# One layer of a hybrid diffusion network on one core: branch rows stored unsplit, the first stage in a written order over all token groups, and the sums of rows behind the context's modulation

## The chip, the cores and the metric

The kernel runs on one core of a Trainium2 chip. The metric is the device time of one execution in microseconds (us). The core's engines are the tensor engine (PE in the profile, with its weight loads shown apart as PEld), the vector engine (DVE), the scalar engine (ACT), GpSimd (POOL) and the sync engine (SP), which here only issues DMAs. ACT and POOL issue DMAs too, in line with their other work; the profile calls these queues SPq, ACTq and POOLq.

## The reference

One layer (DEPTH is 1, D is 1024) is computed for 1024 latent tokens, which lie on a grid 64 wide, and 256 context tokens, 1280 rows in all, with the same weights. Cut to what matters:

```python
sh1, sc1, gt1, sh2, sc2, gt2 = jnp.split(silu(cond) @ w_ada + b_ada, 6, axis=-1)   # one row per stream
u    = rmsnorm(x, g_norm1) * (1 + sc1) + sh1
xp, su, sv, q, k, v, o_pre, gate_pre, br_pre = jnp.split(u @ w_in, points, axis=-1)
y_a  = pool_branch(xp, w_pool, pool_scale, grid)      # window means, minus x, 4 channel groups
y_b  = sgu_branch(su, sv, g_sgu, w_sgu, b_sgu)        # su * (w_sgu @ rmsnorm(sv) + b), chunks of 128
y_c, C_out, n_out, m_out = mlstm_branch(q, k, v, o_pre, gate_pre, ...)   # 4 heads of 128, two directions
branches = jnp.einsum('btrc,rcd->btrd', jnp.stack([y_a, y_b, y_c], axis=2), w_branch)
merged   = jnp.sum(sigmoid(br_pre).reshape(B, T, 3, D) * branches, axis=2)
x  = x + gt1 * (merged @ w_out)
u2 = rmsnorm(x, g_norm2) * (1 + sc2) + sh2
x  = x + gt2 * (jnp.square(relu(u2 @ w_ff1)) @ w_ff2)  # hidden width 4096
return rmsnorm(x, g_final) for both streams, C_out, n_out, m_out of the context
```

All is float32.

## The kernel before

**Products in parts.** Nearly every float32 operand of PE is split into a high half (a cast to a shorter format, `fp32r` in the profile) and a low half (the value less the high half). A product then takes three matmuls: high by high, high by low, low by high (`dense`, `product`). A split is a cast, on ACT or DVE, and a subtraction, on DVE unless said otherwise: `load_w` for a weight of 128x1024, `put_split` for activations, `load_half` and `split` later in the kernel.

**Tokens and tiles.** Tokens form three groups: 0 and 1 are 512 latent tokens each, 2 is the 256 context tokens. Activations lie as 128 channels by up to 512 tokens, in 59 slots of 128x512 (`slot`), with a few rings of smaller count: five tiles `tmp` in the first half of the kernel, and from the gating on the rings `first4`, `six`, `ring` and `tmp2` (four, six, six and six tiles). A ring's tile is handed out again when its last reader is done, so a write into it can wait. `xt[i]` are the ten row tiles of 128 tokens.

**Stages** (times from the start of the span):

- 0 to 92: four blocks of `w_ada` are split and multiplied with the conditioning vectors (`mod_split`), and turned to columns (`mod_cols`), which gives `sh1` and `a1`. The rows are normalised (`norm_rows`: two squarings on ACT, then small steps, among them a power on POOL, then in `scale_rows` one multiplication on DVE), transposed on PE (`transpose_cols`, in the written order `tr(k)` for k from 0 to 7) and modulated on ACT (`modulate_cols`, `mc(k)`). Each modulated tile of groups 0 and 1 is stored to DRAM (`scr_u`) and split. k and v of head 0 for group 0 run in between (tiles `p_k`, `p_v`).
- 92 to 142: the products of the gates (tiles `pg`, weights `wg`), and behind them a chain of small steps on DVE and ACT on 36 rows of 1280 (from L331 to L411, `dmb`), which the four heads need. k, v and q of head 0 run beside it (`head_proj(0)`).
- 142 to 465: four heads. `head(h)` is the matrix memory of one head; `head_proj(h + 1)` is emitted behind it. Each head leaves three tiles `yc` (three groups), stored to `scr_yc` (L582 to L587).
- 465 to 590: pooling (`pool_project`, `pool_window`, `pool_out`) and spatial gating (`spatial`), which leave `ya` and `yb` in the same way (L698 to L701 and L757 to L761).
- 590 to 886: twelve pairs of branch gates, each as seven products of quarters in place of eight (`GatePair`). Their stores go to `scr_g`. Beside them `mod_piece` gathers the rest of the modulation: sums on DVE, a reduction over partitions on POOL, tiles `acc` out of `tmp2`.
- 886 to 1060: the branch products in the order 1, 0, 2 of the branches (loop from L963, products L986 to L988): the rows of a branch are read back, the gates (`sg`) are read back, weights come by `load_half`.
- 1060 to 1210: `project_out` (L1104 to L1110), `modulate_ff(g)` for the three groups (normalise, transpose, modulate for the second half; L1070 to L1084) and `context_out(0..3)`. `quarter_sums(raw2q, ...)` (L715) takes differences of quarters of the modulated rows in place; `split_sum` splits them.
- 1210 to the end: sixteen pairs of the feed-forward's first product (`FeedPair`), then its second (L1340 to L1342).

**What sets the order.** Most of the program goes through a planner, which rearranges the instructions of each engine by modelled times. Instructions issued through `Pinned`, and those in `keep_in_program_order`, keep the written order on their engine:

```python
V, A, G, PE = (Pinned(tc, e) for e in engines)   # from here: written order
...
    V, A, G, PE = engines                        # from here: the planner
```

Before, the pinned part ends behind k and v of head 0 for group 0. Groups 1 and 2, the gates and all that follows are the planner's. DMAs that are issued from `SP` are the planner's too, throughout; those of the modulated tiles are issued from pinned ACT:

```python
        if g < 2:
            A.dma_start(scr_u[g][k], val)
```

The low halves of `w_ada` are made on DVE, but for two of each eight, which POOL makes (`POOL_LO = (2, 5)`). Before, branch rows are split where they are made, stored as halves from ACT, and read as halves into their slots by SP.

Of the kernel before, what the change touches and what calls it, by code (L numbers as in the profile page):

```python
# [14 lines left out]
P = 128  # L15
# [3 lines left out]
T = 1280  # L19
# [10 lines left out]
POOL_LO = (2, 5)  # L30
# [19 lines left out]
def hybrid_step(  # L50
# [100 lines left out]
    scr_ya = dp.tile([2, H, P, T], F32, name="scr_ya")  # L151
    scr_yb = dp.tile([2, H, P, T], F32, name="scr_yb")
    scr_yc = dp.tile([2, H, P, T], F32, name="scr_yc")
# [23 lines left out]
    def modulate_cols(dst, ps, g, k, a, sh, name):  # L177
# [3 lines left out]
        if g < 2:  # L181
            A.dma_start(scr_u[g][k], val)
# [37 lines left out]
    def mod_split(b, ks=range(KT), behind=2):  # L220
# [26 lines left out]

    V, A, G, PE = (Pinned(tc, e) for e in engines)
    scale_rows(0)
    u0 = [None] * KT  # L250

    def tr(k):
        u0[k] = transpose_cols(xt[0:4], 0, k, "u")

    def mc(k):
        modulate_cols(uT, u0[k], 0, k, a1, sh1, "u")

    mod_split(0)
    mod_split(2, (0, 1))
    mod_cols(0)  # L260
# [9 lines left out]
    mod_split(1, (4, 5))  # L270
    mc(1)
    tr(3)
    mod_split(1, (6, 7))
    ps_k0 = ps_mm("p_k00")
    dense(ps_k0, w_k0, uT, 0, (0,))
    mc(2)
    mod_split(3, (0, 1))
    mod_cols(1)
    mod_split(3, (2, 3))
    dense(ps_k0, w_k0, uT, 0, (1,))  # L280
    tr(4)
    tr(5)
    tr(6)
    mod_split(3, (4, 5, 6, 7))
    mc(3)
    w_v0 = load_w(None, "v0", raw_v0)
    mod_cols(3)
    dense(ps_k0, w_k0, uT, 0, (2, 3))
    tr(7)
    ps_v0 = ps_mm("p_v00")  # L290
    dense(ps_v0, w_v0, uT, 0, (0, 1, 2, 3))
# [6 lines left out]
    wgh = wp.tile([P, KT, 100], F32R, tag="hi", name="wg_hi", bufs=NHL)  # L298
    wgl = wp.tile([P, KT, 100], F32R, tag="lo", name="wg_lo", bufs=NHL)
    for i in range(2):  # L300
        ks = slice(4 * i, 4 * i + 4)
        tc.keep_in_program_order(A.copy(wgh[:, ks], wg[i]))
        tc.keep_in_program_order(V.tensor_tensor(wgl[:, ks], wg[i], wgh[:, ks].bitcast(F32), ALU.subtract))
    for i in range(4, NT):
        SP.dma_start(xt[i], xs[i])
    for g in (1, 2):
        scale_rows(g)
        t0, n = GROUPS[g]
        for k in range(KT):
            modulate_cols(uT, transpose_cols(xt[t0 // P : (t0 + n) // P], g, k, "u"), g, k, a1, sh1, "u")  # L310
# [5 lines left out]
    G.dma_start(bgt, bg)  # L316
    G.dma_start(m0t, m0)
    G.dma_start(sel, sel8)
# [3 lines left out]
    for g in range(3):  # L322
        t0, n = GROUPS[g]
        pg = ps_sd(f"pg{g}")
        for k in range(KT):
            ahi, alo = uT[k][g]
            PE.matmul(pg[0:100, :n], wgh[:, k, :], ahi, start=k == 0, stop=False)
# [129 lines left out]
    def proj(idx, name, evict, eng=V):  # L457
        w, ps = begun.pop(name, (None, None))
        w = w or load_w(w_in[idx], name, eng=eng)
        for g in range(3):  # L460
            if ps is None or g > 0:
                ps = ps_mm(f"p_{name}{g}")
                dense(ps, w, uT, g)
            evict(g, ps)
# [1007 lines left out]
```

## Time and profile before

| | |
|---|---|
| median of three runs | 1978.72 us |
| lowest, highest | 1972.24, 1979.62 us |
| time of the profiled execution | 1978.97 us |
| its span, first to last instruction | 1977.2 us |
| mean granted PE clock over the span | 0.99 |
| packets of DMA, bytes | 160382, 328.45 MB |

The span is what the profile shows; the 1.8 us beside it lie around it. In the profile's rows, a line is that of the kernel above; `out<-in` are tiles by name; `x` stands for a count. A matmul or another operation that was issued through `Pinned` has the line of that helper, L44, whatever function wrote it, so such rows are told apart by their tiles. Rows of the timeline begin with the start and the duration in us, and end, in brackets, with how long the engine had been idle and what released it. The granted clock is the share of full speed that PE was given.

### The profile page before, as it was taken

How to read it: one execution, taken by the hardware profiler on the slowest of the kernel's cores; microseconds unless marked ns; L12 is line 12 of the kernel's file. 1: busy time of each engine (PE TensorE's matmuls, PEld its weight loads, DVE VectorE, ACT ScalarE, POOL GpSimd, SP SyncE). 2: the span in 40 equal slices, each digit the busy share in tenths (PEclk: the TensorE clock that was granted, in tenths of full speed). 3: DMA queues.
4: the chain of work that ended last, by engine and by line, in shares of the span. 5: the costliest groups of instructions: out<-in, count | busy, mean ns of one | idle time of the engine just before them, and what ended most of it. 6: DMA issues, size and time to landing. Idle time of an engine off the chain costs nothing.

```text
span 1977.2 us, 28274 instructions
## 1 busy us (share of the span) xinstructions
PE 1916.4 (97%) x10160; PEld 1634.8 (83%) x10160; DVE 1321.5 (67%) x2221; ACT 846.1 (43%) x1732; POOL 383.1 (19%) x372
## 2 busy tenths in 40 slices
PE   5999999999899999999999999999999999999997
PEld 2688888998778888878888888888888878888886
DVE  6684344448878979773566489788876655644664
ACT  6543454653133333331113365545455545443433
POOL 3000001116402324330000005444531110000002
PEclk9999999999999999999999998999999999999999
DMA  8211111112564545359743335777774586655544
GB/s 343 86 46 38 49 59 42 40 57 81 181 224 144 176 139 179 130 194 360 260 129 118 118 123 181 279 257 254 260 262 139 185 322 209 212 169 151 165 133 150
DMA packets 160382, 328.45 MB, mean 166 GB/s; under 512 B 18672, under 2 KB 45168, under 8 KB 158192
## 3 DMA queue, kind: packets, MB, share of 16 engines
q1 hardware_dynamic: 107024, 220.10, 33.9%
q10 hardware_dynamic: 38976, 52.97, 7.4%
q0 software_dynamic: 14240, 53.56, 7.3%
q8 instruction: 80, 1.31, 0.3%
q14 instruction: 62, 0.51, 0.1%
HBM read 225.34 MB, written 101.22 MB: 165 GB/s over the span
## 4 chain that ended last, share of the span: by engine, by line
PE 54%; DVE 3%; issue 1%; ACT 0%; DMA 0%; POOL 0%; ACTq 0%; POOLq 0%; SPq 0%; DVEq 0%
PE w L1340 6%; PE w L1342 6%; PE w L1341 6%; PE fT L830 3%; PE fT L828 3%; PE fT L829 3%; PE pb L986 3%; PE pb L987 3%; PE pb L988 3%; PE fB L830 2%; PE fB L828 2%; PE fB L829 2%; PE po L1104 2%; PE po L1106 2%; PE po L1105 2%; PE fc L828 1%
## 5 line engine op out<-in xcount | busy, mean ns | idle before, releaser
L1179 POOL TENSOR_TENSOR z<-z 128x512 f32<-128x512 f32 x64 | 99.0, 1547 | 122.6 <-DMA z<-in_w_ff 120.1
L885 DVE TENSOR_TENSOR z<-z 128x512 f32<-128x512 f32 x112 | 96.3, 860 | 2.5
L445 POOL PARTITION_ALL_REDUCE acc<-acc x16 | 54.0, 3413 | 188.3 <-DVE acc L439 117.7
L439 DVE SCALAR_TENSOR_TENSOR acc<-z,scond,acc 128x512 f32<-128x512 f32 x112 | 86.0, 816 | 0.0
L1294 POOL TENSOR_TENSOR rs_y<-rs_y,neghalf 128x1 f32<-128x1 f32 x10 | 9.4, 939 | 333.6 <-DVE rs_y L1293 333.5
L1145 ACT ACTIVATE z<-z 128x512 f32<-128x512 f32 x64 | 40.4, 632 | 66.8 <-DVE z L894 31.3
L910 ACT ACTIVATE z<-z 128x512 f32<-128x512 f32 x48 | 30.2, 632 | 72.2 <-DVE z L894 27.5
L819 ACT CAST hi_wb<-raw_wb 128x512 fp32r<-128x512 f32 x24 | 14.8, 621 | 100.1 <-PE pb L987 66.2
L131 POOL TENSOR_TENSOR rs_h<-rs_h,neghalf 128x4 f32<-128x4 f32 (+1 forms) x12 | 11.9, 991 | 207.5 <-DVE rs_h L130 207.4
L992 DVE TENSOR_TENSOR sg<-pb,sg 128x512 f32<-128x512 f32 (+1 forms) x48 | 28.8, 601 | 31.5 <-PE pb L988 31.4
L582 DVE SCALAR_TENSOR_TENSOR yc<-th,ccol,z 128x512 f32<-128x512 f32 (+1 forms) x12 | 7.9, 661 | 57.2 <-PE th L580 57.2
L1146 ACT ACTIVATE z<-z 128x512 f32<-128x512 f32 x64 | 40.3, 629 | 1.1
L1107 DVE TENSOR_TENSOR po<-po,gt 128x512 f32<-128x512 f32 (+1 forms) x24 | 14.6, 607 | 35.5 <-PE po L1106 35.4
L670 POOL TENSOR_TENSOR z<-z 128x1024 f32<-128x1024 f32 (+13 forms) x20 | 34.8, 1750 | 14.1 <-ACT z L654 12.7
L446 POOL TENSOR_TENSOR acc<-acc,bt 1x512 f32<-1x512 f32 x16 | 25.9, 1631 | 58.6 <-issue 58.6
L1170 POOL DMA_DIRECT2D scr_s<-x x48 | 26.4, 550 | 55.6 <-DVE x L1164 49.6
L1110 ACT ACTIVATE po<-z 128x512 f32<-128x512 f32 (+1 forms) x24 | 12.7, 529 | 48.4 <-DVE z L1109 34.1
L44 PE MATMUL pm<-wah,shl 128*4 128x512 f32 x32 | 14.9, 485 | 16.7 <-DVE s_x L44 12.8
L516 DVE SCALAR_TENSOR_TENSOR z<-z,dmb,kv 128x129 f32<-128x129 f32 x56 | 16.3, 345 | 21.9 <-PE kv L505 21.6
L569 DVE TENSOR_TENSOR den<-den,gcol 128x2 f32<-128x2 f32 x40 | 6.2, 159 | 35.2 <-ACT den L568 34.5
L993 DVE TENSOR_TENSOR z<-z,sg 128x512 f32<-128x512 f32 (+1 forms) x48 | 28.8, 601 | 1.3
L990 DVE TENSOR_TENSOR z<-pb,sg 128x512 f32<-128x512 f32 (+1 forms) x24 | 14.1, 600 | 22.1 <-PE pb L988 17.7
(5093 smaller groups left out, 7311.5 us busy)
## 6 DMA issues: line engine op xcount, KB each, us to landing
z<-in_w_ff SPq DMA_DIRECT2D x64, 512.0 KB, 5.4
z<-in_w_ada SPq DMA_DIRECT2D x64, 256.0 KB, 3.1
scr_t<-z POOLq DMA_DIRECT2D x16, 1024.0 KB, 4.6
z<-in_w_in SPq DMA_DIRECT2D x24, 512.0 KB, 4.4
scr_g<-z ACTq DMA_DIRECT2D x48, 256.0 KB, 2.0
sg<-scr_g SPq DMA_DIRECT2D x48, 256.0 KB, 4.5
scr_h<-z ACTq DMA_DIRECT2D x48, 256.0 KB, 3.9
scr_s<-x POOLq DMA_DIRECT2D x48, 256.0 KB, 3.3
```

Source lines behind the costliest of these rows:

```text
L439: V.scalar_tensor_tensor(acc[j], raw, scond[:, k, j : j + 1], acc[j], ALU.mult, ALU.add)
L828: PE.matmul(ps, whi[:, s], ahi, start=first and k == ks[0], stop=False)
L829: PE.matmul(ps, whi[:, s], alo, start=False, stop=False)
L830: PE.matmul(ps, wlo[:, s], ahi, start=False, stop=end and k == ks[-1])
L885: V.tensor_tensor(out, x, y, op)
L986: PE.matmul(pb[:, :n], whi[:, s], yh, start=kc == 0, stop=False)
L987: PE.matmul(pb[:, :n], whi[:, s], yl, start=False, stop=False)
L988: PE.matmul(pb[:, :n], wlo[:, s], yh, start=False, stop=kc == 3)
L1179: G.tensor_tensor(out, x, y, ALU.subtract)
L1340: PE.matmul(banks[j], h_[:, s], rh, start=fp == 0, stop=False)
L1341: PE.matmul(banks[j], l_[:, s], rh, start=False, stop=False)
L1342: PE.matmul(banks[j], h_[:, s], rl, start=False, stop=fp == NFP - 1)
```

## The change

1. `scr_ya`, `scr_yb`, `scr_yc` hold one copy of each row, unsplit. The three places that make them store one tile each, from SP. Each branch reads its twelve tiles into `tmp2` and splits them there, with a cast on ACT and a subtraction on DVE.
2. `POOL_LO` goes: DVE makes all low halves of `w_ada`. The stores of the modulated tiles are issued from POOL's queue.
3. `scale_rows` becomes `row_stats` and `row_apply`. The loads of row tiles 4 to 7 come ahead of those of the gate weights; row tiles 8 and 9, the gate weights and q's weight of head 0 are fetched within the pinned part.
4. The pinned part is written in another order and runs on over groups 1 and 2: transpositions four steps ahead of the products, modulations two ahead, and k, v and q of head 0 as the products. The gate products of groups 0 and 1 stand ahead of the steps of group 2, those of group 2 last. `proj` and `head_proj` take up what is then begun; the gate weights' halves move from the weight rings into slots.
5. `quarter_sums(raw2q)` runs whole behind `modulate_ff(2)`; before, its first half stood between `context_out(2)` and `context_out(3)`.

The products, their number and their shapes are the same. The diff, cut:

```diff
-POOL_LO = (2, 5)
...
-    scr_ya = dp.tile([2, H, P, T], F32, name="scr_ya")
+    scr_ya = dp.tile([H, P, T], F32, name="scr_ya")
...
         if g < 2:
-            A.dma_start(scr_u[g][k], val)
+            nc.gpsimd.dma_start(scr_u[g][k], val)
...
-    def scale_rows(g):
-        for i in range(GROUPS[g][0] // P, (GROUPS[g][0] + GROUPS[g][1]) // P):
-            r = norm_rows(xt[i], 1, f"x{i}")
-            V.tensor_scalar(xt[i], xt[i], r[:, 0:1], None, ALU.mult)
+    def row_stats(i):
+        row_rstd[i] = norm_rows(xt[i], 1, f"x{i}")
+
+    def row_apply(i):
+        V.tensor_scalar(xt[i], xt[i], row_rstd[i][:, 0:1], None, ALU.mult)
...
-    wg = [slot(f"wg{i}", F32)[:, 0:400].rearrange("p (k c) -> p k c", c=100) for i in range(2)]
-    for i in range(2):
-        SP.dma_start(wg[i], w_gate[:, 4 * i : 4 * i + 4, :])
+    for i in range(4, 8):
+        SP.dma_start(xt[i], xs[i])
...
-            (G if k in POOL_LO else V).tensor_tensor(wl, ada[b, k], wh.bitcast(F32), ALU.subtract)
+            V.tensor_tensor(wl, ada[b, k], wh.bitcast(F32), ALU.subtract)
...
     mod_split(0)
-    mod_split(2, (0, 1))
-    mod_cols(0)
+    mod_split(2)
+    w_k0 = load_w(None, "k0", raw_k0)
+    raw_q0 = fetch_w(w_in[I_Q], "q0")
...
     tr(0)
     tr(1)
     tr(2)
-    mod_split(2, (2, 3, 4, 5, 6, 7))
-    mod_split(1, (0, 1))
+    mod_split(1, (0, 1, 2))
+    mod_cols(0)
     mod_cols(2)
-    mod_split(1, (2, 3))
-    w_k0 = load_w(None, "k0", raw_k0)
+    mod_split(1, (3,))
     mc(0)
...
     for k in (4, 5, 6, 7):
-        mc(k)
+        if k < 6:
+            mc(k + 2)
+            row_apply(k)
+        if k == 4:
+            row_stats(7)
         dense(ps_k0, w_k0, uT, 0, (k,))
         dense(ps_v0, w_v0, uT, 0, (k,))
-    begun = {"k0": (w_k0, ps_k0), "v0": (w_v0, ps_v0)}
-    V, A, G, PE = engines
...
+    row_apply(6)
+    row_apply(7)
+    w_q0 = load_w(None, "q0", raw_q0)
...
+    begun = {nm: (w, []) for nm, w in (("k0", w_k0), ("v0", w_v0), ("q0", w_q0))}
+    ps_q0 = ps_mm("p_q00")
+    dense(ps_q0, w_q0, uT, 0, range(0, 4))
+    steps = [(g, k) for g in (1, 2) for k in range(KT)]
+    for k in range(4):
+        tr(k, 1)
+    mc(0, 1)
+    mc(1, 1)
+    dense(ps_q0, w_q0, uT, 0, range(4, 8))
+    for at, (g, k) in enumerate(steps):
...
+        if (g, k) == (2, 0):
+            gates_of(0)
+            gates_of(1)
+        if at + 4 < len(steps):
+            tr(steps[at + 4][1], steps[at + 4][0])
+        if at + 2 < len(steps):
+            mc(steps[at + 2][1], steps[at + 2][0])
+        if k == 0:
+            begun["k0"][1].append(evict_kqv("k", 0, g - 1, ps_k0, kq0))
+            begun["v0"][1].append(evict_kqv("v", 0, g - 1, ps_v0, kq0))
...
+        dense(ps_k0, w_k0, uT, g, (k,))
+        dense(ps_v0, w_v0, uT, g, (k,))
...
+    gates_of(2)
+    V, A, G, PE = engines
...
-            part = [tmp(f"yc{h}_{g}_{i}", F32R)[:, :n] for i in range(2)]
-            put_split(part, yc[:, :n])
-            for i in range(2):
-                A.dma_start(scr_yc[i, h, :, t0 : t0 + n], part[i].bitcast(F32))
+            SP.dma_start(scr_yc[h, :, t0 : t0 + n], yc[:, :n])
...
-            part = [tmp(f"ya{gi}_{g}_{i}", F32R)[:, :n] for i in range(2)]
-            sc = ccol[:, C_PS + gi : C_PS + gi + 1]
-            A.activation(part[0], ps[:, :n], AF.Copy, scale=sc)
-            V.scalar_tensor_tensor(part[1], ps[:, :n], sc, part[0].bitcast(F32), ALU.mult, ALU.subtract)
-            for i in range(2):
-                A.dma_start(scr_ya[i, gi, :, t0 : t0 + n], part[i].bitcast(F32))
+            ya = tmp(f"ya{gi}_{g}")
+            A.activation(ya[:, :n], ps[:, :n], AF.Copy, scale=ccol[:, C_PS + gi : C_PS + gi + 1])
+            SP.dma_start(scr_ya[gi, :, t0 : t0 + n], ya[:, :n])
...
-            part = split_part(f"yb{ci}", g)
-            put_split(part, mix[g][:, :n])
-            for i in range(2):
-                A.dma_start(scr_yb[i, ci, :, t0 : t0 + n], part[i].bitcast(F32))
+            SP.dma_start(scr_yb[ci, :, t0 : t0 + n], mix[g][:, :n])
...
-                part = split_part(f"y{r}_{kc}", g)
-                for i in range(2):
-                    SP.dma_start(part[i].bitcast(F32), scr[i, kc, :, t0 : t0 + n])
-                ys[kc].append(part)
+                raw = tmp2(f"yr{r}_{kc}_{g}")
+                SP.dma_start(raw[:, :n], scr[kc, :, t0 : t0 + n])
+                hi, lo = split_part(f"y{r}_{kc}", g)
+                A.copy(hi, raw[:, :n])
+                V.tensor_tensor(lo, raw[:, :n], hi.bitcast(F32), ALU.subtract)
+                ys[kc].append((hi, lo))
...
-    quarter_sums(raw2q, (0, 1))
     context_out(3)
...
     modulate_ff(2)
-    quarter_sums(raw2q, (2, 3))
+    quarter_sums(raw2q)
```

More of the change, by code (lines that the diff above doesn't have):

```diff
@@ L313, in hybrid_step, with evict_kqv @@
+    row_apply(7)
+    w_q0 = load_w(None, "q0", raw_q0)
+    kq0 = slot("kq0", F32)
+    def evict_kqv(nm, h, g, ps, kq):
+        n = GROUPS[g][1]
+        if g == 2 and nm != "v":
+            t = kq[:, 0:256] if nm == "k" else kq[:, 256:512]
+        else:
+            t = slot(f"{nm}T{h}_{g}", F32)
+        A.activation(t[:, :n], ps[:, :n], AF.Copy, scale=float(P) ** -0.5 if nm == "k" else 1.0)
+        return t
     bgt = cp.tile([36, 2], F32, name="bgt")
@@ L455, in hybrid_step, with proj @@
     hn2 = [z[:, 9010 + i * 512 : 9522 + i * 512].rearrange("p (c t) -> p c t", t=P) for i in range(2)]
-    def proj(idx, name, evict, eng=V):
-        w, ps = begun.pop(name, (None, None))
+    def proj(idx, name, evict, eng=V, w=None, groups=range(3)):
         w = w or load_w(w_in[idx], name, eng=eng)
[L460 to L463, printed above, removed]
+        for g in groups:
+            ps = ps_mm(f"p_{name}{g}")
+            dense(ps, w, uT, g)
             evict(g, ps)
```

123 lines of the change are left out of this document (69 added, 54 removed).

## Prediction

> **What bounds the kernel now.** I read the page's totals first, then the time by stage, then what the tensor engine (PE) waited for, then the order of time where it waited.
>
> ```profile
> span 1977.2 us, 28274 instructions
> PE 1916.4 (97%) x10160; PEld 1634.8 (83%) x10160; DVE 1321.5 (67%) x2221; ACT 846.1 (43%) x1732; POOL 383.1 (19%) x372
> ```
>
> ```profile
> 12.80:60.00 47.20, 39.84 (x180) 22.77 (x181) 36.95 (x60) 32.48 (x63) 13.53 (x12) 0.93 0.80 313
> 60.00:92.00 32.00, 27.67 (x141) 19.29 (x140) 19.03 (x48) 14.36 (x30) 2.43 (x4) 1.00 0.17 66
> 92.00:142.00 50.00, 47.20 (x264) 41.19 (x262) 42.91 (x47) 24.24 (x28) 2.47 (x5) 0.93 0.15 46
> 142.00:490.00 348.00, 347.05 (x2265) 315.70 (x2265) 169.93 (x433) 169.78 (x484) 50.05 (x42) 1.00 0.16 53
> 490.00:600.00 110.00, 99.95 (x514) 82.46 (x513) 84.34 (x122) 33.88 (x57) 25.99 (x28) 0.97 0.54 188
> 860.00:900.00 40.00, 37.81 (x179) 31.67 (x178) 21.22 (x30) 11.72 (x21) 11.54 (x7) 0.96 0.82 273
> 900.00:1150.00 250.00, 250.00 (x1261) 213.16 (x1260) 140.53 (x245) 56.81 (x114) 8.52 (x15) 1.00 0.54 190
> 1150.00:1215.00 65.00, 59.88 (x390) 54.68 (x389) 60.47 (x124) 46.52 (x99) 16.87 (x8) 0.92 0.36 125
> ```
>
> The columns of the stages are the stretch, its length, then busy time of PE, its weight loads, DVE, ACT and POOL, the granted clock, the DMA share and GB/s. PE is the bound, 97% busy, and the change adds and removes no product: every gain has to come out of PE's 60.8 us of idle time (1977.2 less 1916.4) and out of the stretches at half clock. Of the idle time 12.8 us lie before the first product, and after it the change touches five places: 7.4 us up to 60, 4.3 up to 92, 2.8 up to 142, 10.1 in the pooling and gating stage (490 to 600), 2.2 where the branch products begin, 5.1 around the sums. From 142 to 490 and from 900 to 1150 PE has no idle time worth naming.
>
> ```profile
> PE pm L44 <- ACT wah L44: 3.9, 1, 3.9
> PE p_su L124 <- ACT xp L639: 3.4, 1, 3.4
> PE pt L1078 <- ACT xn L1070: 3.0, 1, 3.0
> PE fB_g L828 <- ACT a_g0h L810: 2.6, 1, 2.6
> 32.00:40.00 8.00, 4.33 (x14) 1.92 (x15) 6.09 (x10) 4.20 (x8) 1.28 (x1) 0.57 1.03 414
> 520.00:528.00 8.00, 4.75 (x14) 3.75 (x15) 3.82 (x7) 5.01 (x9) 1.89 (x1) 0.79 0.40 140
> ```
>
> The waits are single and short, 2.6 to 3.9 us, but behind them the clock falls to half: 43% and 21% of 8 us are missing in the last two rows, 3.4 and 1.7 us, and 7% of the 50 us from 92 to 142, 3.5 us. Where PE works in that time it is lost too, so a wait of 3 us is worth about 5.
>
> **First stage, token group 0** (to 60 us).
>
> ```profile
> 12.15 5.74 ACT L44 CAST wah<-wa 128x512 fp32r<-128x512 f32 x10
> 29.03 0.57 ACT L44 COPY mrow_hi<-pm 4x512 f32<-4x512 f32 x1 [1.68 <-PE pm L44]
> 31.55 0.78 ACT L44 ACTIVATE val_u<-pt_u,sh,a 128x512 f32<-128x512 f32 x1
> 34.60 0.35 ACTq L44 DMA_DIRECT2D scr_u<-val_u  x1
> 35.00 1.14 ACT L44 CAST wah<-wa 128x512 fp32r<-128x512 f32 x2 [2.67 <-DMA wg<-in_w_gate]
> 36.04 0.77 ACT L44 ACTIVATE val_u<-pt_u,sh,a 128x512 f32<-128x512 f32 x1
> 59.38 0.39 PE L44 MATMUL p_v<-u7h,lo_v 128*128 128x512 f32 x1
> L44 DVE TENSOR_TENSOR wal<-wa,wah 128x512 fp32r<-128x512 f32 x24 | 20.4, 904 | 1.3 <-ACT wah L44 1.3
> L44 POOL TENSOR_TENSOR wal<-wa,wah 128x512 fp32r<-128x512 f32 x8 | 11.3, 1412 | 20.1 <-ACT wah L44 19.8 <-PE pt_u L44 0.3
> L44 DVE TENSOR_TENSOR u3l<-val_u,u3h 128x512 fp32r<-128x512 f32 x1 | 0.7, 693 | 0.0
> L1170 POOL DMA_DIRECT2D scr_s<-x x48 | 26.4, 550 | 55.6 <-DVE x L1164 49.6
> ```
>
> The value of 31.55 is ready at 32.33, yet its store leaves ACT's queue at 34.60: it waited there for an earlier load, 2.67 us, and the next casts, the second modulation (36.04) and PE's 3.9 us stand behind it. The change takes these stores off ACT. Its new list up to the second modulation is 21 casts of 0.574 from 12.15 (24.2), the cast of w_k0 (1.1 as two of them), two row copies (1.1) and the first modulation (0.8): 27.3; plus the 2.5 us that before lie between the second row copy (29.03) and the modulation it releases (31.55): 29.8 in place of 36.04, 6.2 us earlier.
>
> All 32 low halves now fall to DVE. That is 8 more by 0.693, 5.5 us; but the 24 it had cost 904 ns beside POOL and 693 is what the same shape costs alone, so 24 x 0.211 = 5.1 us come back: nil. The 8 POOL instructions of 1412 ns go. What is moved ahead of the stage's end is row work of group 1: four statistics (ACT, in its idle time) and two row multiplications of 1024 columns on DVE, 2.8 us as four subtractions. The loads of rows 4 to 7 move ahead of those of the gate weights in SP's queue; the gate products come after group 1, so this costs nothing, unless the rows land late, and then at most what the row work was moved ahead by. 59.8 - 6.2 + 2.8: the last product of group 0 ends 3.4 us earlier, at 56.4.
>
> The 16 stores cost POOL 0.55 each (the row of scr_s): 8.8 us in an engine busy 13.5 of 47 us, of which the 11.3 above go; but the powers that scale the rows now queue among them. On what they do to DVE and back, the Trainium skill, "SBUF — State Buffer", section "SBUF: two separate sides", holds against this edit: a store issued from GpSimd cannot write its descriptors while DVE runs in a two-port mode, 0.62 us becoming some 3.1 us. By that figure the 8 stores of group 0 would be an estimated 25 us of POOL. The 550 ns mean of the 48 scr_s stores doesn't show it, and I go by that row.
>
> **Groups 1 and 2, the products of head 0, the gates.**
>
> ```profile
> 24.22 1.53 PE L44 MATMUL pt_u<-cst,z 128*128 128x128 f32 x12
> 92.13 0.28 PE L124 MATMUL p_k<-u0c,hi_k 128*128 128x256 f32 x1
> 94.44 0.42 DVE L331 COPY z<-pg 36x256 f32<-36x256 f32 x1
> 103.34 0.40 PE L124 MATMUL p_q<-u0h,hi_q 128*128 128x512 f32 x1
> 108.81 0.39 PE L124 MATMUL p_q<-u0h,hi_q 128*128 128x512 f32 x1
> 142.17 0.32 DVE L411 COPY dmb<-pd 128x160 f32<-128x160 f32 x1
> ```
>
> 24 products of 512 columns take 5.47 us (103.34 to 108.81), 0.228 each; k of group 2 with v of groups 1 and 2 takes 11.21 (92.13 to 103.34), so a 256-column product is 0.12. Between 59.8 and 92 PE had 72 of the first (16.4), 24 of the second (2.9) and 48 transpositions of 0.13 (6.1): 25.4 of 32.2 us, 6.8 lost, to rows not yet scaled and to modulations. In the new order rows 4 to 7 are scaled in advance, transpositions run four ahead and modulations two, and q0's 24 products stand between. For each k PE has six products and four transpositions, 1.9 us, DVE a cast and a subtraction, 1.1, ACT one modulation, 0.8: PE is the slowest. I leave 1.8 us of waits, for lo_q0 behind two row multiplications and for the evictions behind the gate products: 5 us gained, with the 3.4 above 8.4. By then PE has also done the 11.21 and 5.47 us, 16.7, that used to follow the gates. The gates so end at about 92.1 + 16.7 - 8.4 = 100.4. **I take 8.5 us**, with bounds of 2 (only ACT's stalled store goes) and 16 (all 7.4, 4.3 and the half clock).
>
> Against it stands the chain of small gate steps on DVE and ACT: 94.44 to 142.5, 48 us, before head 0 can be transposed. PE covered it with the 16.7 us and with the rest of q0 and o0. Now the chain starts at 102 and the cover is the rest of q0 (5.47 + 2.9), o0, and k, v of head 1 (13.8 each): 49.8 us. It suffices if the planner brings in head 1's products. The idle 2.8 us and the half clock of this stretch are a matter of where it puts the gate's transpositions. **I take 1 us gained**; from 5 (both gone) to a loss of 29 (only q0 and o0 as cover, 26 idle, 3.4 at half clock).
>
> **Rows stored unsplit.**
>
> ```profile
> L699 DVE SCALAR_TENSOR_TENSOR ya<-pp,ccol,ya 128x512 fp32r<-128x512 f32 (+1 forms) x12 | 7.9, 658 | 4.5 <-ACT ya L698 4.5
> 523.25 0.50 PE L124 MATMUL p_su<-u0h,hi_su 128*128 128x512 f32 x1 [3.39 <-ACT xp L639]
> 521.59 0.93 ACTq L701 DMA_DIRECT2D scr_ya<-ya  x2
> 522.62 0.58 ACT L639 COPY xp<-p_xp 128x512 f32<-128x512 f32 x1 [1.71 <-DVE mt L750]
> ```
>
> Of 72 stores 36 are left, on SP instead of ACT. In the pooling stage 12 DVE subtractions (7.9 us) and the 12 casts with 12 subtractions of the yb rows go, the latter at most 0.693 each and the casts less: some 20 of DVE's 84 us. What PE gets is one place: at 522.62 ACT copies out a finished product only after the stores queued ahead of it (521.59) have left, and PE waits 3.4 us and then runs at half clock, 5.1 in all. **I take 4**; 8.6 if the wait of fB_g (2.6 and 1.7) goes too, and a loss of 2 if SP's loads stand behind a store that waits for DVE. In the heads yc's splits go as well, worth nothing: PE loses 1 us in 348. There, each yc store on SP keeps the next weight load waiting until DVE is done; that PE waits for no load in 348 us is the cover, and if it were gone each of the 12 stores would cost its DVE lag, some 2 us.
>
> **Rows split when read.** Each branch gets 12 loads for 24, then 12 casts on ACT and 12 subtractions on DVE: 36 of each, by 0.574 and 0.693 some 21 us of ACT and 25 of DVE. Branches 0 and 2 are read beside PE-bound products with DVE busy 140 of 250 us: nothing. The first branch stands at the front:
>
> ```profile
> 878.91 1.21 POOL L447 DMA_DIRECT2D scr_mod<-acc  x2
> 883.81 0.86 SPq L817 DMA_DIRECT2D raw_wb<-in_w_branch  x2
> ```
>
> Before, the weights of the first product are loaded at 883.81, behind 24 row loads, and PE loses 2.2 us, and 4% of 40 us to the clock. Now the row loads go through the ring of six tmp2 tiles, which the last accumulators hold until their store of 878.91 lands. Fewer loads speak for a gain of up to 4, the ring for a loss of up to 8. **I take 0.**
>
> **Sums behind the modulation.**
>
> ```profile
> 1184.87 0.68 DVE L715 TENSOR_TENSOR u2r<-u2r,u2r 128x512 f32<-128x512 f32 x1
> ```
>
> A sum of 0.68 runs just ahead of the step that starts the context's modulation, for which PE waits 3.0 us. With all sums behind it that step comes one or two sums, 0.7 to 1.4 us, earlier; but DVE is busy 60.5 of these 65 us, and the splits that need the sums end as late. **I take 0.5**, from 4 (wait and half clock gone) to a loss of 1.5.
>
> **The sum.** The profiled execution took 1978.97 (span 1977.2), the median of the runs is 1978.72. 1978.97 - 8.5 - 1 - 4 - 0 - 0.5 = 1965.0. Not all terms reach an end together; this case alone runs from 1954 to 1976.
>
> **Rivals.**
> Slower: *the gate chain lies bare.* k, v and half of q of head 0 are spent before the gates. For it speaks the 48 us chain; against it that head 1's products were ready early. Without them, 1978.97 - 13 + 29 = 1995; it decides from some 23 us without cover, that is if neither k1 nor v1 comes. 0.10.
> No change: *the gain is given back.* The chain ends some 8 us later than before, and the four heads follow one another; if they can't be done faster, what PE did early is missing as filler in the last head, 8 to 9 us: 1973.5. For it: head 0 can't start earlier. Against: PE was never idle in the heads. 0.13.
> No change: *the ring of six* delays the first branch by the full 8 us: 1973. 0.09.
> No change: *POOL's queue holds the row powers.* If a store beside DVE costs what POOL's subtraction did, 1.4 us, eight of them put the scaling of rows 4 to 7 up to 11 us back, and the 5 us of groups 1 and 2 with 2 more are lost: 1972. 0.06. The Trainium skill's rule on such stores, named above, would act in this way.
>
> The likeliest case has 0.62. A difference under 0.5%, 9.9 us, can't be told from none here. Faster by more means below 1968.8: 0.50 of the likeliest case and 0.08 of the three middle rivals, 0.58. Slower means above 1988.6: 0.08 of the first rival and 0.02 beside, 0.10. The rest, 0.32, is no change. The range of 1951 to 1986 leaves out the far end of the bare chain and a gain from all bounds at once.
>
> **What would show it.** Right: the second modulation near 30 us, the last product of group 0 near 56, gates done near 100 with head 0's k and v behind them, no wait of p_su for ACT near 520. Wrong: PE waiting for pc or tk between 120 and 150, new idle time before 480, branch products waiting for yr's splits near 886, POOL powers late near 55.

## The result, and the profile after

The changed kernel takes 1951.73 us (median of four runs, 1949.12 to 1952.31) against 1979.17 before (1972.24 to 1984.41): a ratio of 0.986 (0.983 to 0.989), 27.4 us faster. The forecast was 14, to 1965.0. The profiled execution of the changed kernel took 1952.31 us. Its totals on the page, and then the stretches shown of before (length, then busy time of PE, weight loads, DVE, ACT, POOL, granted clock, DMA share, GB/s):

```profile
span 1950.5 us, 28164 instructions
PE 1905.8 (98%) x10160; PEld 1628.3 (83%) x10160; DVE 1295.9 (66%) x2205; ACT 863.2 (44%) x1767; POOL 381.1 (20%) x380
```

```profile
12.80:60.00 47.20, 43.40 (x199) 25.86 (x199) 36.64 (x71) 32.79 (x63) 8.62 (x13) 0.96 0.83 325
60.00:92.00 32.00, 30.54 (x154) 23.62 (x153) 14.75 (x33) 14.46 (x30) 6.07 (x10) 1.00 0.17 67
92.00:142.00 50.00, 47.90 (x282) 42.17 (x280) 39.55 (x41) 21.77 (x28) 2.46 (x5) 1.00 0.13 43
142.00:490.00 348.00, 343.27 (x2248) 311.35 (x2247) 170.69 (x430) 173.22 (x487) 57.77 (x53) 1.00 0.14 45
490.00:600.00 110.00, 108.16 (x591) 91.47 (x590) 75.81 (x110) 36.87 (x64) 15.26 (x17) 1.00 0.49 165
860.00:900.00 40.00, 39.64 (x199) 33.23 (x198) 27.18 (x48) 17.50 (x32) 2.73 (x3) 1.00 0.92 320
```

PE is fuller in the first stretch and from 490 to 600 (108.16 of 110 us for 99.95), and emptier in the heads, 142 to 490 (343.27 of 348 for 347.05).

Since stages shift, a time lost by stage says more. PE does the same products in every kernel here. Each matmul is counted at its usual distance to the next one (0.227 us for 512 columns, 0.120 for 256, 0.11 for 128); this work adds up to 1881.4 us, and what the span has beyond it, waits and half clock alike, is lost. The bounds are set by the work done, at 75, 200, 450, 530, 806 and 830 us of it, which in the kernel before are 110, 242, 494, 593, 874 and 902 us of the span. One profiled execution of each kernel, in us lost:

| kernel | to the gates | gate chain | heads | pooling | gate pairs | first branch | rest of the products | after the last product |
|---|---|---|---|---|---|---|---|---|
| before | 35.2 | 6.6 | 2.1 | 19.3 | 4.6 | 4.1 | 12.9 | 11.2 |
| after | 26.3 | 5.6 | 6.1 | 7.0 | 5.9 | 0.9 | 9.4 | 7.9 |
| e1 rows only | 36.1 | 6.7 | 2.0 | 5.0 | 4.8 | 0.9 | 12.0 | 11.2 |
| e2 first stage only | 26.2 | 4.7 | 8.1 | 22.6 | 5.1 | 3.4 | 12.8 | 7.9 |
| e3 sums only | 35.6 | 5.5 | 2.1 | 19.3 | 5.9 | 3.4 | 12.2 | 11.2 |
| e4 rows stored from ACT | 25.4 | 4.5 | 11.6 | 12.7 | 4.2 | 0.8 | 11.4 | 7.9 |
| e5 halves stored from SP | 36.4 | 6.9 | 2.1 | 17.4 | 4.9 | 3.9 | 12.3 | 11.2 |
| e6 modulated rows from ACT | 36.1 | 5.6 | 6.1 | 7.0 | 0.7 | 0.8 | 10.7 | 11.2 |
| e7 low halves on POOL | 29.6 | 5.7 | 6.0 | 7.1 | 5.5 | 1.0 | 11.1 | 7.9 |
| e8 four and four banks | 25.9 | 5.7 | 13.8 | 15.9 | 2.9 | 0.9 | 12.6 | 7.9 |
| e9 DVE's work kept | 25.7 | 6.2 | 7.6 | 9.6 | 5.9 | 0.6 | 13.4 | 7.9 |
| e10 q0 behind the gates | 36.4 | 6.2 | 5.0 | 7.0 | 5.8 | 1.0 | 11.4 | 8.8 |
| e11 more on POOL | 35.6 | 7.0 | 2.1 | 17.1 | 3.0 | 1.0 | 12.6 | 11.2 |
| e12 casts on ACT | 26.0 | 5.6 | 6.0 | 7.1 | 0.8 | 0.7 | 9.2 | 7.9 |

From before to after: 8.9 to the gates, 1.0 in their chain, 4.0 lost in the heads, 12.3 in the pooling stage, 1.3 lost in the gate pairs, 3.2 in the first branch, 3.5 in the rest, 3.3 behind the last product: 26.9, against 26.7 between the spans (1977.2 and 1950.5). How far a column can be trusted shows in two rows. e11 is the kernel before with a few fills on POOL and the same order on PE and ACT: it differs from before by 3.1 us in the first branch and 2.2 in the pooling stage. e3 has the order of before on PE, ACT and DVE, and differs from it by up to 1.3. The gate pairs go from 0.7 to 5.9 in kernels that differ nowhere near them. The profiled executions of e4, e6 and e12 happened to be 5.6, 3.7 and 4.0 us faster than the medians given below, so their rows add up to less than the medians say.

The steps of the first stage in the trace after (start, duration):

```profile
30.25 0.78 ACT L43 ACTIVATE val_u<-pt_u,sh,a 128x512 f32<-128x512 f32 x1
55.06 0.40 PE L43 MATMUL p_v<-u7h,lo_v 128*128 128x512 f32 x1
102.54 0.28 PE L43 MATMUL pg<-u7c,wgl 128*100 128x256 f32 x1
150.28 0.32 DVE L475 COPY dmb<-pd 128x160 f32<-128x160 f32 x1
L181 POOL DMA_DIRECT2D scr_u<-val_u x16 | 9.9, 619 | 27.5 <-ACT val_u L43 26.8 <-DVE rs_x L43 0.3 <-issue 0.2
L43 DVE TENSOR_TENSOR wal<-wa,wah 128x512 fp32r<-128x512 f32 x32 | 20.0, 685 | 0.0
```

The second modulation stands at 30.25 (29.8 forecast), the last product of group 0 ends near 55.5 (56.4), the gates end at 102.8 (100.4), the gate chain at 150.6, 8 us later than before, as forecast. What PE waits for in the whole span, the rows that matter (total, times, longest):

```profile
PE pt L1124 <- ACT xn L1116: 3.0, 1, 3.0
PE pc L460 <- DVE z L448: 2.1, 1, 2.1
PE p_k L123 <- ACT z L579: 1.8, 1, 1.8
PE p_xp L123 <- DVE mt L804: 1.3, 1, 1.3
```

The waits of p_su for xp (3.4) and of fB_g for its cast (2.6) are gone; that of pt for xn stands unchanged at 3.0; p_k's is new. Two of the signs that the prediction named for being wrong are there: PE waits for pc near 140 (2.1 us; before, 2.8), and it has new idle time before 480 (p_k).

### The profile page after: what moved, and what is told of

It is laid out like the page before. It is cut to its first block, busy times and chain, and to the rows that moved or that the text cites. A ratio compares the mean times of both kernels' runs of the same rounds, so it can differ in the third digit from the quotient of the medians.

```text
span 1950.5 us, 28164 instructions
## 1 busy us (share of the span) xinstructions
PE 1905.8 (98%) x10160; PEld 1628.3 (83%) x10160; DVE 1295.9 (66%) x2205; ACT 863.2 (44%) x1767; POOL 381.1 (20%) x380
## 4 chain that ended last, share of the span: by engine, by line
PE 54%; DVE 3%; issue 1%; ACT 0%; DMA 0%; POOL 0%; ACTq 0%; POOLq 0%; DVEq 0%
PE w L1385 6%; PE w L1386 6%; PE w L1387 6%; PE fT L874 3%; PE fT L872 3%; PE fT L873 3%; PE pb L1033 3%; PE pb L1032 3%; PE pb L1034 3%; PE fB L874 2%; PE fB L872 2%; PE fB L873 2%; PE po L1152 2%; PE po L1151 2%; PE po L1150 2%; PE fc L874 1%
## 5 line engine op out<-in xcount | busy, mean ns | idle before, releaser
L510 POOL TENSOR_TENSOR acc<-acc,bt 1x512 f32<-1x512 f32 x16 | 24.0, 1515 | 56.4 <-issue 56.4
L1156 ACT ACTIVATE po<-z 128x512 f32<-128x512 f32 (+1 forms) x24 | 12.7, 529 | 48.4 <-DVE z L1155 34.2
L569 DVE SCALAR_TENSOR_TENSOR z<-z,dmb,kv 128x129 f32<-128x129 f32 x56 | 16.3, 345 | 26.2 <-PE kv L558 26.1
L43 PE MATMUL pm<-wah,shl 128*4 128x512 f32 x32 | 13.8, 461 | 13.8 <-ACT wah L43 13.8
```

## The experiments

All times are medians, with the ratio to the kernel before, run beside them on the same chip, and its interval. The changed kernel's 1951.73 is from another session, in which the kernel before took 1979.17; beside the experiments it took 1976.95 to 1977.98. A difference to 1951.73 is therefore good to some 2 us.

**Each part alone.** e1 takes the edits of `scr_ya`, `scr_yb`, `scr_yc` and of the reading into the kernel before; e2 the first stage (parts 2 to 4 of the change), e3 the move of the sums.

> The kernel before with part 1 of the change alone: rows stored unsplit from SP, split when read. Theory: the pooling stage's gain (12 us, from the first product of xp's last half to the first branch gate's) belongs to this part, and the first branch's 3 us with it, and the heads lose nothing: about 15 us faster than before, 1964; the wait of p_su for ACT (3.4) and that of fB_g for its cast (2.6) are gone. Rival 1, the heads' new waits (4 us) come from the row stores on SP: then they stand here too, and the gain is 11. Rival 2, the pooling stage gained because the order of the stage ahead was another: then this gains 5 or less.

> The kernel before with the first stage of the change alone (parts 2 to 4). Theory: about 9 us ahead where the gates' chain begins, and 4 of them lost again in the heads, where PE, a product further ahead, waits for banks that the sigmoid's copies hold; the pooling stage loses what it lost before: about 5 us faster, 1974. Rival 1 (the heads' waits belong to the row stores): 9 us faster, 1970. Rival 2 (the pooling stage's gain comes from here): 17 us, 1962.

> The kernel before with the move of the sums alone. Theory: the wait of the context's first transposition (3.0 us for ACT) stays, and the waits of the first feed-forward products for the split sums go: 2 us faster, 1977, all of it between 1200 and 1215. Rival, the 2 us there come from the rest of the change, by another order of the planner: no difference, 1979.

e1: 1960.45 (0.991; 0.990 to 0.993), 17 us faster. The pooling stage gains 14.3, the first branch 3.2, the heads lose nothing. e2: 1972.43 (0.998; 0.997 to 0.998), 5.4 us faster. 9.0 are gained to the gates and 3.3 behind the last product, 6.0 are lost in the heads, and 3.3 in the pooling stage, where the old stores stand. e3: 1977.87 (1.000; 0.999 to 1.001), no difference: the rival was right. Its trace says why: the sixteen sums start between 1160.2 and 1184.9 us, as in the kernel before, and PE, ACT and DVE have the order of before throughout. The planner had put the sums there already, so moving them in the source moved nothing. e1 and e2 give 22.7 of the 27.4, whose interval reaches from 21 to 34; the first stage is worth 5.4 us alone, and with the sums 8.7 on top of e1.

**What gave the pooling stage its time.** Three things changed there at once: the queue of the stores (ACT to SP), DVE's work, and the tiles that halves hold until their store has landed, with twice the stores. e4 and e5 change the queue, e9 the work:

```diff
 e4 (from after)
-            SP.dma_start(scr_yb[ci, :, t0 : t0 + n], mix[g][:, :n])
+            A.dma_start(scr_yb[ci, :, t0 : t0 + n], mix[g][:, :n])
 ... the same for scr_ya and scr_yc
 e5 (from before)
-                A.dma_start(scr_yb[i, ci, :, t0 : t0 + n], part[i].bitcast(F32))
+                SP.dma_start(scr_yb[i, ci, :, t0 : t0 + n], part[i].bitcast(F32))
 ... the same for scr_ya and scr_yc
 e9 (from after), ahead of the store; likewise for yc, and the second line for ya
+            V.tensor_scalar(mix[g][:, :n], mix[g][:, :n], 1.0, None, ALU.mult)
+            V.tensor_tensor(mix[g][:, :n], mix[g][:, :n], mix[g][:, :n], ALU.max)
```

> The changed kernel with its unsplit row stores on ACT's queue instead of SP's. Theory of the queue: copies and casts stand in ACT behind stores that wait for DVE, as before; about half of the pooling stage's 12 us is lost again, 1958. Rival, DVE's relief (20 us of subtractions gone): the stage keeps its gain, 1952.

> The kernel before with its stores of halves on SP's queue instead of ACT's; the splits stay where they were, and 24 loads a branch. Theory of the queue and DVE's relief together: the queue alone gives half of the pooling stage's gain, some 6 to 8 us, and the first branch, with all its loads, gains nothing: 1971. Rival, the queue alone is the cause: 12 to 14 us in the pooling stage, 1965. Rival, the relief alone: no gain, 1978.

> The changed kernel with the DVE work of the removed splits put back as idle operations in place (a multiplication by one and a maximum of a tile with itself on each yc and yb tile, the maximum on each ya tile), so that DVE does as much as before but no tile is held for it. Theory of the room (halves take twice the tiles, and each is held until its store has landed; ACT then waits for a free tile): the pooling stage keeps 10 us or more of its 12, and the time is within 2 us of the changed kernel's 1952. Rival, DVE's relief: the stage falls back to a gain of 2 to 4 us, 1960.

e4: 1967.15 (0.994; 0.993 to 0.996). e5: 1976.58 (1.000; 0.999 to 1.001). e9: 1957.57 (0.990; 0.988 to 0.992). Of the 12.3 us, e4 keeps 6.6, e5 has 1.9, e9 keeps 9.7. The time of e5 fits neither of its readings (1971 and 1965). e9 falls short of its theory by 0.3 us in the stage and by 4 in the time. e4 loses more than its theory's 1958, because its heads lose 11.6 us for 6.1: there PE waits up to 3.4 us for the sigmoid. What ACT waits for in the pooling stage tells more. First ACT's own rows in the kernel before, and two of DVE's:

```profile
506.56 0.68 ACT L698 ACTIVATE ya<-pp,ccol 128x512 fp32r<-128x512 f32 x1
507.27 0.33 ACTq L701 DMA_DIRECT2D scr_ya<-ya  x1
513.46 0.41 DVE L115 CAST yb0h<-mt 128x512 fp32r<-128x512 f32 x1
513.91 0.33 ACTq L761 DMA_DIRECT2D scr_yb<-yb0h  x1
515.53 0.74 DVE L699 SCALAR_TENSOR_TENSOR ya<-pp,ccol,ya 128x512 fp32r<-128x512 f32 x1
516.30 0.33 ACTq L701 DMA_DIRECT2D scr_ya<-ya  x1
516.73 0.69 ACT L698 ACTIVATE ya<-pp,ccol 128x512 fp32r<-128x512 f32 x1 [9.49 <-DMA scr_yb<-yb0h]
```

Then, in e5, the longest of these waits and ACT's next copy of `xp`, with SP's store ahead of them:

```profile
513.68 0.38 SPq L701 DMA_DIRECT2D scr_ya<-ya  x1
520.44 0.69 ACT L698 ACTIVATE ya<-pp,ccol 128x512 fp32r<-128x512 f32 x1 [11.80 <-DMA scr_ya<-ya]
523.00 0.59 ACT L639 COPY xp<-p_xp 128x512 f32<-128x512 f32 x1 [0.84 <-DMA scr_yb<-yb0h]
```

Last, the sums of ACT's waits in e5, in e4 and in e9:

```profile
ACT ya L698 <- DMA scr_ya<-ya: 17.8, 5, 11.8
```

```profile
ACT a_g0h L854 <- DVE mt L804: 6.7, 1, 6.7
ACT hi_su L93 <- DVE mt L804: 5.8, 1, 5.8
```

```profile
ACT ya L749 <- DMA scr_yb<-mt: 5.0, 3, 3.3
```

Before, ACT stands for 9.49 us ahead of a `ya` (its earlier piece came at 506.56). The bracket names the store of `yb0h`, but that store cannot be the cause: it was issued at 513.91 and landed 4.7 us later, at 518.6, when ACT was running again. ACT stood behind two stores in its own queue, each waiting for DVE. The store of `yb0h` leaves 0.04 us after DVE's cast has ended (513.87), that of the low half of `ya` 0.03 us after DVE's subtraction (516.27), and the next `ya` follows it. The store of the earlier `ya`, issued at 507.27, had landed after 2.0 us.

With the halves stored from SP (e5) ACT's queue is no longer in the way, and now ACT does wait for stores to land, 17.8 us in five pieces: `ya` needs two tiles of the ring of five for each of its three groups, and a tile is free only when its store has landed. In the longest piece the value was done at 508.64, but SP issued its store at 513.68, behind loads, and the store took 6.7 us to land.

With one tile per row and the stores on ACT (e4) no such wait for a landing is left in these rows; there the casts of the next weights stand behind a store that waits for DVE's `mt`. With the DVE work put back and one tile per row stored from SP (e9) most of the gain stays. So it takes both, rows stored whole and the stores off ACT; either alone gives 6.6 and 1.9 of 12.3. DVE's relief, the other reading, is 2.6 of it at most; what else e9 is slower by lies in the heads (7.6 for 6.1) and in the rest of the products (13.4 for 9.4). What makes halves dear once they are off ACT, the tiles that they hold or the number of their stores, no run separates: none has a longer ring.

**What the first stage hangs on.** e6 puts the stores of modulated rows back on ACT, e7 puts eight of the low halves back on POOL.

```diff
 e6 (from after)
-            nc.gpsimd.dma_start(scr_u[g][k], val)
+            A.dma_start(scr_u[g][k], val)
 e7 (from after)
+POOL_LO = (2, 5)
-            V.tensor_tensor(wl, ada[b, k], wh.bitcast(F32), ALU.subtract)
+            (G if k in POOL_LO else V).tensor_tensor(wl, ada[b, k], wh.bitcast(F32), ALU.subtract)
```

> The changed kernel with the stores of the modulated rows back on ACT. Theory: ACT's next casts stand behind them again, and of the 9 us ahead at the gates' chain some 4 to 6 go; the heads give back less for it, so that the end is 2 to 4 us later, 1955. POOL's last drain, 2.5 us in the kernels with the new first stage and 7.6 without: if the number of stores on POOL sets it, it is 7.6 here and the time 3 us longer still, 1958. Rival, the new order alone makes the stores harmless: 1952.

> The changed kernel with eight of the 32 low halves of the modulation's weights back on POOL. Theory (the prediction's: what DVE is spared it loses to slower subtractions): the same within 1 us at the gates' chain, 1952, with POOL's last drain unchanged. Rival: POOL's 1.4 us a subtraction are late for PE in the new order, 2 to 4 us, 1955. If these POOL instructions set the last drain, it is 7.6 us and the end 5 us later.

e6: 1964.88 (0.994; 0.992 to 0.995), 13 us slower than the changed kernel and slower than all its readings, though POOL's drain is 7.6 us as one of them had it. SP's loads of rows, ACT, and PE's longest waits in e6:

```profile
28.44 2.21 SPq L203 DMA_DIRECT2D z<-in_xs  x4
28.56 0.78 ACT L43 ACTIVATE val_u<-pt_u,sh,a 128x512 f32<-128x512 f32 x1 [2.93 <-DVE a L43]
36.08 0.36 ACTq L43 DMA_DIRECT2D scr_u<-val_u  x1
36.48 0.62 ACT L43 CAST wah<-wa 128x512 fp32r<-128x512 f32 x1 [7.14 <-DMA z<-in_xs]
```

```profile
PE pm L43 <- ACT wah L43: 20.4, 2, 11.9
```

The store leaves ACT 6.7 us after its value is done, where before it was 2.3, and PE waits 8.5 us for the cast behind it (20.4 less the first wait of 11.9; 1.3 in the changed kernel). It is a load that holds the store. In the trace the DMAs of SP and ACT take eight semaphores in turn, which tell that a DMA has landed; this store has the one that SP's second load of rows had, and leaves when that load has landed, at 36.01. Before, the store of 34.60 shares one with a load of the gate weights that landed at 34.52. The DMAs of POOL have eight semaphores of their own, so a store there waits for none of SP's loads. The whole gain to the gates is gone (36.1 lost, before 35.2): the new order gains nothing with the stores on ACT. e7: 1957.03 (0.990; 0.988 to 0.991), 5.3 slower. The rival's 2 to 4 us came, 3.3 to the gates, but not by POOL's halves being late. PE's waits for low halves and the subtractions that make them (least, median and longest in ns), in e7 and in the changed kernel:

```profile
PE pm L44 <- DVE wal L44: 4.7, 4, 3.1
L44 DVE TENSOR_TENSOR wal<-wa,wah x24: 677/683/1781, 15.3 to 46.6; 128x512 fp32r<-128x512 f32 x24
L44 POOL TENSOR_TENSOR wal<-wa,wah x8: 1262/1629/2147, 13.6 to 43.3; 128x512 fp32r<-128x512 f32 x8
```

```profile
PE pm L43 <- DVE wal L43: 0.9, 1, 0.9
L43 DVE TENSOR_TENSOR wal<-wa,wah x32: 682/684/690, 14.3 to 43.6; 128x512 fp32r<-128x512 f32 x32
```

All of these waits are for halves that DVE makes, not POOL. In e7 five of DVE's 24 subtractions take 1.76 to 1.78 us in place of 0.68, each while a subtraction runs on POOL. One of the five makes the first half that PE needs, and PE waits 3.1 us for it; two of the other three waits end with one of the five too.

**What the heads lose.** In the changed kernel's trace, DVE, ACT and PE around the new wait of p_k:

```profile
272.89 0.74 DVE L635 SCALAR_TENSOR_TENSOR yc<-th,ccol,z 128x512 f32<-128x512 f32 x1
273.66 0.60 ACT L579 ACTIVATE z<-p_o 128x512 f32<-128x512 f32 x1 [0.65 <-DVE yc L635]
274.31 0.50 PE L123 MATMUL p_k<-u0h,hi_k 128*128 128x512 f32 x1 [1.77 <-ACT z L579]
```

The products of o for the next head are done, and hold their banks until the sigmoid can write over `so`, which `yc` of the head before still reads. e8 gives the products a fourth bank, e10 leaves q0 to the planner.

```diff
 e8 (from after)
-        return pp.tile([P, 512], F32, tag="mm", name=name, bufs=3)
+        return pp.tile([P, 512], F32, tag="mm", name=name, bufs=4)
-        return pp.tile([P, 512], F32, tag="sd", name=name, bufs=5)
+        return pp.tile([P, 512], F32, tag="sd", name=name, bufs=4)
 e10 (from after)
-    w_q0 = load_w(None, "q0", raw_q0)
...
-    dense(ps_q0, w_q0, uT, 0, range(0, 4))
...
-    dense(ps_q0, w_q0, uT, 0, range(4, 8))
```

> The changed kernel with four banks for products and four for the rest, in place of three and five. Theory (in the heads the finished products of o hold two or three of three banks until the row step of the head before has read the sigmoid's tile): with a fourth bank the waits of p_k and sv behind p_o (1.9 and 1.3 us) go, and the lead of 9.8 us at the heads' start is still 8 or more at their end: 2 to 4 us faster, 1949. Rival, ACT's order is what holds them: the waits stay, and the fewer banks for the small steps cost some us: 1952 to 1957.

> The changed kernel with q's products of head 0, group 0, left to the planner behind the gates instead of standing in the pinned part. Theory (the heads lose 4 to 5 us because products done ahead of the gates are missing as filler, so that o of the next head is through early and holds its banks): the gates' chain starts 5 us earlier and ends 5 us earlier, the heads lose 2 us or less, and groups 1 and 2 lose 2 to 3 us for want of q's products: 1951. Rival, the heads lose what they lose by the planner's order alone: 4 us again, and with what groups 1 and 2 lose 1955.

e8: 1965.38 (0.994; 0.992 to 0.995). It is slower than both its readings (1949; 1952 to 1957). The 1.8 us of p_k go, but sv then waits 6.3 us in all for 2.2, and the pooling stage, where mx and pp now wait for ya (4.1 and 2.4), loses 8.9 more: the small steps need their fifth bank. e10: 1963.94 (0.993; 0.992 to 0.995), where its readings had 1951 and 1955. It lost its time elsewhere: the planner put the cast of q's weight among the pinned casts of `w_ada`, on ACT ahead of a load that came late:

```profile
46.59 1.04 ACT L93 CAST hi_q<-raw_q 128x1024 fp32r<-128x1024 f32 x1 [8.52 <-DMA raw_q<-in_w_in]
```

p_k's wait of 1.8 is gone there too, and the heads lose 5.0 for 6.1. So this one wait comes from the banks that o holds, and needs q0 ahead. But it is 1.8 of 4.0. For the rest e6 rules one reading out: it starts its heads with no lead at all and loses the same 6.1, with the same rows of waits as the changed kernel. It isn't the lead in time that is given back; it is the order that follows from the new first stage. The other 2 us stand for the most part in two more waits, of sv for the same sigmoid (1.1) and of p_k for ACT's `kT` (0.7); which part of the order brings them stays open, and that the prediction's rival (what PE did early is missing as filler) names it was not shown.

**Two smaller questions.** POOL's drain, an instruction of the program's end, begins with its last power and takes 7.6 us in the kernel before and 2.5 after. e11 adds 16 fills on POOL, without a DMA, to the kernel before; e12 moves the twelve casts of the second half's modulated rows from DVE to ACT.

```diff
 e11 (from before)
-    cp.tile([P, 24], F32, name="pad1")
+    spare = cp.tile([P, 24], F32, name="pad1")
+    for i in range(16):
+        nc.gpsimd.memset(spare[:, i : i + 1], 0.0)
 e12 (from after)
-                    V.tensor_copy(hi, rf)
+                    A.copy(hi, rf)
```

> The kernel before with 16 more instructions on POOL at its start (fills of one column each), no further DMA. POOL's last drain was 7.6 us in the five kernels with 640 to 654 POOL instructions and 169 DMAs, 2.5 us in the five with 666 to 681 and 185. If the number of instructions sets it: 2.5 us, and the end 3.3 us earlier. If the number of DMAs: 7.6.

> The changed kernel with the twelve casts of the modulated rows of the second half (u2h, 0.42 us each on DVE) on ACT. From 1150 to 1215 DVE is busy 60.7 of 65 us and ACT 37.6, and the context's rows wait for DVE: 5 us less on DVE ahead of them. Theory (DVE bounds this stage): the wait for xn (3.0 us) goes or shrinks to under 1, and with it the half clock: 3 to 5 us faster, 1948. Rival (ACT's queue takes up what DVE gives): the same within 1 us, 1952.

e11: the drain is 7.6 us, so the number of instructions doesn't set it (one run, 1972.6). e12: 1950.47 (0.986; 0.985 to 0.988), which can't be told from the changed kernel's 1951.73. The wait stays:

```profile
PE pt L1124 <- ACT xn L1116: 2.5, 1, 2.5
```

## Why the prediction was right or wrong

The time stands 0.7 us inside the fast end of the range, 1951. That it lies inside is luck: the terms that came out larger than forecast would have carried it past that end but for the loss in the heads, which the sum had at nothing.

**First stage, 8.5: 8.9 measured, one sub-step wrong, so partly luck.** ACT's store ahead of the casts was the mechanism (e6), and it waited for a load, as was read. The step "the 8 POOL instructions of 1412 ns go ... nil" was not nil. DVE's busy time is as worked out (32 subtractions at 685 ns, forecast 693), but the 904 ns in the mean were a few subtractions of 1.8 us among many of 0.68, and PE waits for the long ones: 3.3 us by e7 to the gates and 5.3 at the end. The steps that were counted thus brought some 5.6 of their 8.5, and this one 3.3. Only busy times were added up, not who waits.

**Stores on POOL: the row was right.** The 16 stores cost 619 ns in the mean, 0.81 us at most, 550 ns forecast, and PE waits for no power in this stage. The Trainium skill, "SBUF — State Buffer", section "SBUF: two separate sides", has some 3.1 us for a store from GpSimd beside a DVE copy. None of these 16 came near it on POOL; whether any of DVE's work beside them was in the two-port mode that the page names, no run shows.

**Gate chain, 1: right, 1.0.** It ended 8 us later, and head 1's products covered it, as the sum had it. The rival of a bare chain did not come.

**Heads, 0: wrong, 4.0 lost.** The prediction gave this loss a rival of its own, with 8 to 9 us. It came in half, and the lead given back was not its cause (e6). The step "PE loses 1 us in 348", taken to go on as it was, did not hold: with q0 ahead, PE waits 2.9 us for the sigmoid of o, which it does not in e10.

**Pooling stage, 4: wrong, 12.3.** This is the term that was mis-sized most. The prediction took the one wait of p_su and its half clock for the gain, laid both to the stores queued on ACT, and kept fB_g's wait for the bound of 8.6. Before, the stage had five waits of PE of 1.2 to 3.4 us (p_su, p_xp twice, fB_g, mx); 1.3 of p_xp's and 0.4 of fB_g's are left. The mechanism, ACT behind its stores, is what the trace before shows; the step "what PE gets is one place" failed. ACT stood behind stores that waited for DVE ahead of `ya` too (9.49 us), and the price left out that halves taken off ACT still hold it up: e5, which moves the queue alone, gains no more there (1.9) than e11 does by chance (2.2), because ACT then waits for tiles until stores have landed. With rows stored whole the same move brings 5.7 (12.3 less the 6.6 of e4).

**Rows split when read, 0, with a gain of up to 4 as a bound: 3.2 in this execution.** The kernels that read whole rows lose 0.6 to 1.0 in the first branch, nine of nine; those that read halves 3.4 to 4.1 in four of five, and in e11 1.0. So the gain is there in most executions; the delay by the ring of six did not come.

**Sums, 0.5: nothing.** The step that was to bring it, an earlier modulation of the context, did not happen. In the changed kernel, too, a sum runs just ahead of that step:

```profile
1164.89 0.68 DVE L762 TENSOR_TENSOR u2r<-u2r,u2r 128x512 f32<-128x512 f32 x1
```

pt waits for xn 3.0 us as before, in e3 too, and e3's sums start when those of before do. The place in the source was read as the place in the order, which is the planner's. The 3.5 us that the changed kernel gains in the rest of the products are not shown to come from any edit: the seven kernels made from it lose 9.2 to 13.4 there, and it 9.4.

**Not in the sum: 3.3 us behind the last product.** All kernels with the stores of modulated rows on POOL have them (e10 2.4 of them), e2 among them, those without don't, e6 among them.

The forecast of 14 us in all thus held a first stage whose sum came out, and had a loss of 4 in the heads only as a rival. It missed some 8 in the pooling stage, and 3 each in the first branch, in the rest of the products and at the end; the gate pairs took 1.3 back.

## What to carry to other kernels

A store waits in line on the engine that issues it, until its value is made and, here, until an unrelated load that shares its semaphore has landed; every cast behind it waits too. Moving it to an engine without work for PE can be worth more than the work it saves. A tile that is stored holds its room until the store has landed: where a ring is short, ask how many tiles each result takes. Both show as idle time of the engine that fills the tiles; where a DMA is named as the releaser, check that it had landed by then, and look at what that engine's queue issued last. Busy times that cancel on one engine are not a price: ask who waits for the longest. And where a planner sets the order, look in the trace whether an edit moved anything.

## What was not expected of the hardware

POOL's drain at the end of the program is 7.60 or 7.61 us in the six kernels with 169 DMAs issued on POOL and 2.46 in the eight with 185; nothing else that was tried moves it (640 to 681 instructions on POOL). SP's last stores of the output are issued at these times, before and after:

```profile
1970.57 0.39 SPq L1299 DMA_DIRECT2D out_y<-z  x1
```

```profile
1947.12 0.38 SPq L1344 DMA_DIRECT2D out_y<-z  x1
```

From there to the end of the span it is 6.6 us before and 3.4 after. Before, SP is done at 1973.1 and all engines wait for POOL until 1976.4; after, POOL is done at 1947.8 and they wait for SP until 1949.7. Whether it is the number of DMAs or which ones was not tried.

The clock fell to half behind a wait of 2.1 us. The changed kernel around its wait of pc, the last row within the two before it:

```profile
139.00:142.00 3.00, 0.90 (x8) 0.47 (x6) 2.80 (x11) 0.00 (x0) 1.07 (x2) 1.00 0.01 0
142.00:145.00 3.00, 3.00 (x24) 2.62 (x23) 3.00 (x5) 0.21 (x1) 0.00 (x0) 0.73 0.00 0
145.00:148.00 3.00, 3.00 (x11) 2.34 (x11) 2.94 (x10) 1.87 (x2) 0.00 (x0) 0.70 0.21 35
143.40:146.70 3.30, 3.30 (x9) 2.63 (x8) 3.30 (x7) 1.53 (x3) 0.00 (x0) 0.50 0.00 0
```

PE is idle for 2.1 us and pays 3 x 0.27 and 3 x 0.30, 1.7 us, behind it. The Trainium skill, "TensorE: Matmul & The Clock Gate", section "HAM oscillation — how this bites in real kernels", puts the abstract bound at gaps above some 3.4 us; here a shorter one was enough. A wait of 1.8 us did it in one kernel and not in another. These are the rows around p_k's wait in the changed kernel and in e9, with the same busy time of PE:

```profile
272.00:276.00 4.00, 2.23 (x11) 1.67 (x10) 3.70 (x10) 3.32 (x4) 0.00 (x0) 1.00 0.45 94
276.00:280.00 4.00, 4.00 (x19) 3.28 (x18) 2.67 (x4) 2.79 (x10) 0.00 (x0) 1.00 0.26 102
```

```profile
272.00:276.00 4.00, 2.23 (x9) 1.60 (x8) 4.00 (x12) 3.32 (x5) 0.00 (x0) 0.85 0.35 131
276.00:280.00 4.00, 4.00 (x15) 3.19 (x14) 3.00 (x5) 2.57 (x9) 0.00 (x0) 0.72 0.17 66
```

The 4 x 0.15 and 4 x 0.28 us, 1.7 in all, are what e9 loses more in the heads than the changed kernel (7.6 for 6.1), within 0.2. What decides between the two no run shows.
